# Hybrid attention and retention trunk: block corners, GpSimd pieces, adding transfers and the grouping of the FFN blocks

## The chip, the cores and the metric

The kernel runs on one core of a Trainium2 chip. The metric is device time in microseconds (us) of one execution. An execution of this program was also taken by the profiler, and its instructions, DMA packets and semaphores are what the views below are made from. TensorE (PE; its weight loads are PEld), VectorE (DVE), ScalarE (ACT), GpSimd (POOL) and SyncE (SP, which issues most DMA transfers) each work through a queue of their own in order.

## The reference

A decoder trunk of two layers on 512 tokens of width 1024, with 16 learned meta tokens in front (528 positions). All is float32.

```
h = concat(meta, x)                                        # (528, 1024)
for each of 2 layers:
    xn   = rmsnorm(h) ;  proj = xn @ w_in                  # 1024 x 3592
    fox  = 8 heads of 64: softmax(q k^T / 8 + c_t - c_s, causal) v,  c = cumsum(log sigmoid(gate))
    ret  = 4 heads of 128: rotary, sum over s<=t of gamma^(t-s) (q_t k_s) v_s, group norm, times silu(gate)
    h   += concat(fox, ret) @ w_out                        # 1024 x 1024
    hn   = rmsnorm(h)
    h   += (silu(hn @ w_gate) * (hn @ w_up)) @ w_down      # 1024 x 2816 x 1024
return rmsnorm(h) without the meta positions
```

In the second layer only the 512 real positions are needed behind the keys and values.

## The kernel before

**Layout and precision.** `h` lies transposed, eight tiles of 128 channels by 528 positions. Every float32 product is made as three products of a high and a low part (`hi*hi`, `hi*lo`, `lo*hi`): ScalarE rounds a tensor to its high part, and VectorE or GpSimd subtracts it from the original for the low part (`split`, line 126; `convert`, line 149, for the weights). TensorE's order is written out by hand as a list of steps (a plan), and the Tile framework orders the other engines' instructions in advance, by a model of their costs; each engine then runs its queue as it stands.

**Attention.** A dense step is one 128-channel piece of the contraction (`dense_steps`, line 180). While it runs, the next weight tile is converted in two halves of four pieces, at steps 1 and 4 (`ahead`). Where a job has `pool` set, GpSimd makes the low half of 128 x 512 elements in one instruction (line 177). The steps of the forgetting attention (`fox_steps`) and the retention (`ret_steps`) are merged between dense steps. A fox head takes its 512 real queries in blocks b = 0 to 3 of 128 (and the meta queries as b = -1 in layer 0). `scores` writes the probabilities of block b into the tile `p_tiles[b]`, with 16 + 128(b+1) keys and zeros behind them. `turn` (line 526) transposes them with TensorE in 128-key pieces 0 to b+1; the last piece holds 16 keys. Only the last 16 queries of the block can see those, so of this piece a corner of 16 x 16 is not zero. ScalarE and VectorE split the transposed pieces into `pth` and `ptl`, and `product` multiplies them by the values.

**FFN.** The 22 blocks of 128 FFN columns run in `ROUNDS`. The first `PLAIN` blocks of a layer are plain: gate and up product, each eight steps of full width. Every other block is a `Unit`: gate and up are made together by a scheme of seven instead of eight half-size products, on the two halves of the contraction (HB = 4 pieces each) and of the positions (w = 264 or 256). Its weights are four jobs: `make1` (the gate tile `a` itself), `make2` (S: the sum of the up tile's halves, and that minus a's first half), `make3` (a's first half minus b's) and `make4` (a's second half minus S). `load` fetches `a` and `b` by SP. The inputs' sums are made by `x_forms` (line 816), four times per layer, with tiles `S` of two buffers which `make2` uses too; their places among the plan's steps are fixed, before steps 12, 20, 28 and 36 of the FFN. `need` converts a job and up to two behind it. Converted weights lie in two rings of two buffers (`whi/wlo` and `fwhi/fwlo`), in turn. When a round is done, its down products are filled into the units of the next one, one pair of output pieces per unit: half of it in the middle, half after the unit's last product. The last round's down products stand alone; in the last layer they run in two column parts, and the closing norm is placed between their pieces (`after_a` to `after_7`).

The names the prediction uses: line 200 is the dense steps' matmul, 401 the transposes, 552 the attention's product with the values, 860 the units' matmul, 995 the down products', 177 the low halves, 849 the units' low parts, 894 and 895 the sums in `make2`, 901 the one in `make3`, 283 the end of a norm's Newton step, 1169 the closing norm's high part, 1091 its sums, 1095 its output products.

## Time and profile before

| | |
|---|---|
| three timed runs | 1282.78, 1283.13, 1283.19 us; median 1283.13 |
| profiled execution | span 1282.4 us; the median of the runs is 0.7 us above it |
| mean granted TensorE clock | 0.996 |
| busy: PE, DVE, ACT, POOL | 1265.5, 1013.6, 691.4, 177.3 us |
| HBM read / written | 116.91 MB / 2.13 MB |

A busy time is the union of an engine's instructions, so a matmul's modelled end that overlaps the next one counts once. The page and the other views name an instruction by its line, engine, operation and tiles (`out<-in`). "idle before" and "waited for" name what ended an engine's idle time.

### The profile page before, as it was taken

The page shows a single profiled execution, that of the slowest core. Times are in us where ns is not written, and L with a number is a line of the kernel's source. Part 1 is how long each engine was busy: PE and PEld are TensorE (multiplying, and loading weights), DVE is VectorE, ACT ScalarE, POOL GpSimd, SP SyncE. Part 2 cuts the span into 40 slices and gives each one's busy share as a digit, 9 for nine tenths or more (in the row PEclk, how much of TensorE's full clock was granted, in tenths as well). Part 3 has the DMA queues.
Part 4 walks back from the last instruction along what each step waited for, and adds up shares of the span by engine and source line. Part 5 has one row for each costly group of instructions (what it writes and reads, how often), then busy time and mean ns, then how long its engine had stood idle before and what let it go on. Part 6 is the DMA issues. An engine that isn't in the chain of part 4 may idle for free.

```text
span 1282.4 us, 23297 instructions
## 1 busy us (share of the span) xinstructions
PE 1265.5 (99%) x9335; PEld 1205.4 (94%) x9335; DVE 1013.6 (79%) x1828; ACT 691.4 (54%) x1246; POOL 177.3 (14%) x145
## 2 busy tenths in 40 slices
PE   9999999999999999999999999999999999999997
PEld 8899999999999999999999989999789999999996
DVE  7877856879988887887686878568899878888866
ACT  6666655676444444444455665457765444444444
POOL 1233333210000000000014334333000000000000
PEclk9999999999999999999999999999999999999998
DMA  6222222123333333332323122222223322332321
GB/s 231 76 67 84 75 84 84 60 68 121 109 98 99 99 99 99 100 99 83 99 76 117 59 99 84 75 92 67 99 78 129 106 99 99 99 100 99 105 77 66
DMA packets 45676, 120.54 MB, mean 94 GB/s; under 512 B 5360, under 2 KB 12272, under 8 KB 45568
## 3 DMA queue, kind: packets, MB, share of 16 engines
q1 hardware_dynamic: 45136, 118.77, 28.2%
q8 instruction: 73, 1.20, 0.4%
q14 instruction: 35, 0.29, 0.1%
q10 hardware_dynamic: 432, 0.29, 0.1%
HBM read 116.91 MB, written 2.13 MB: 93 GB/s over the span
## 4 chain that ended last, share of the span: by engine, by line
PE 88%; DVE 7%; ACT 3%; DMA 1%; issue 1%; DVEq 0%; ACTq 0%
PE psd L200 27%; PE psa L860 18%; PE psd L995 14%; PE psd L860 13%; PE psa L995 4%; PE psa L200 4%; PE psa L401 2%; PE psa L490 2%; PE psa L552 1%; PE psa L709 1%; PE psa L679 1%; DMA bc<-cdr 1%; ACT whi L176 0%; DVE qs L421 0%; DVE kl L435 0%
## 5 line engine op out<-in xcount | busy, mean ns | idle before, releaser
L177 POOL TENSOR_TENSOR wlo<-raw,whi 128x512 fp32r<-128x512 f32 x126 | 171.8, 1377 | 386.0 <-ACT whi L176 384.8
L200 PE MATMUL psd<-xh,whi 128*128 128x264 f32 (+1 forms) x792 | 196.6, 316 | 0.8 <-ACT whi L176 0.8
L200 PE MATMUL psd<-xh,wlo 128*128 128x264 f32 (+1 forms) x792 | 187.2, 304 | 0.0
L200 PE MATMUL psd<-xl,whi 128*128 128x264 f32 (+1 forms) x792 | 186.5, 303 | 0.4 <-DVE xl L303 0.4
L200 PEld LDWEIGHTS psd<-xh,whi 128*128 128x128 f32 x792 | 128.9, 190 | 5.6 <-ACT whi L176 1.5
L200 PEld LDWEIGHTS psd<-xh,wlo 128*128 128x128 f32 x792 | 127.5, 189 | 6.4 <-DVE wlo L177 0.4
L200 PEld LDWEIGHTS psd<-xl,whi 128*128 128x128 f32 x792 | 128.2, 190 | 4.7 <-DVE xl L303 0.8
L176 ACT CAST whi<-raw 128x512 fp32r<-128x512 f32 (+1 forms) x168 | 98.2, 614 | 38.2 <-PE psd L200 18.0
L848 ACT CAST whi<-raw 128x1024 fp32r<-128x1024 f32 (+2 forms) x62 | 54.9, 885 | 51.3 <-PE psd L860 40.0
L848 ACT CAST fwhi<-raw 128x1024 fp32r<-128x1024 f32 (+2 forms) x62 | 55.6, 897 | 47.5 <-PE psd L860 40.0
L849 DVE TENSOR_TENSOR wlo<-raw,whi 128x1024 fp32r<-128x1024 f32 (+2 forms) x62 | 62.9, 1014 | 11.3 <-ACT whi L848 10.9
L849 DVE TENSOR_TENSOR fwlo<-raw,fwhi 128x1024 fp32r<-128x1024 f32 (+2 forms) x62 | 64.0, 1032 | 9.0 <-ACT fwhi L848 8.7
L860 PE MATMUL psa<-th,whi 128*128 128x264 f32 (+1 forms) x232 | 65.5, 282 | 0.0
L860 PE MATMUL psa<-th,wlo 128*128 128x264 f32 (+1 forms) x232 | 65.4, 282 | 0.0
L860 PE MATMUL psa<-tl,whi 128*128 128x264 f32 (+1 forms) x232 | 65.3, 282 | 0.0
L510 ACT ACTIVATE pdNone<-pdNone,nmax 128x144 f32<-128x144 f32 (+1 forms) x64 | 36.9, 576 | 50.4 <-DVE nmax L497 33.6
L860 PE MATMUL psa<-th,fwhi 128*128 128x264 f32 (+1 forms) x224 | 63.4, 283 | 0.0
L860 PE MATMUL psa<-tl,fwhi 128*128 128x264 f32 (+1 forms) x224 | 63.3, 283 | 0.0
L860 PE MATMUL psa<-th,fwlo 128*128 128x264 f32 (+1 forms) x224 | 63.3, 282 | 0.0
L128 DVE TENSOR_TENSOR ptl<-psa,pth 128x512 fp32r<-128x512 f32 (+4 forms) x88 | 41.9, 490 | 26.9 <-ACT pth L127 26.9
L926 ACT COPY e<-psa 128x264 f32<-128x264 f32 (+1 forms) x114 | 42.8, 375 | 28.4 <-PE psa L860 24.1
L848 ACT CAST fwhi<-S 128x1024 fp32r<-128x1024 f32 x20 | 21.0, 1049 | 68.6 <-PE psa L860 66.5
(339 smaller groups left out, 4031.7 us busy)
## 6 DMA issues: line engine op xcount, KB each, us to landing
raw<-w_in SPq DMA_DIRECT2D x54, 512.0 KB, 3.5
raw<-w_gate SPq DMA_DIRECT2D x44, 512.0 KB, 3.9
fraw<-w_up SPq DMA_DIRECT2D x38, 512.0 KB, 3.5
raw<-w_down SPq DMA_DIRECT2D x64, 256.0 KB, 2.7
raw<-w_out SPq DMA_DIRECT2D x16, 512.0 KB, 3.5
raw<-w_down SPq DMA_DIRECT2D x32, 192.0 KB, 2.4
bc<-cdr SPq DMA_DIRECT2D x16, 264.0 KB, 3.2
raw<-w_up SPq DMA_DIRECT2D x6, 512.0 KB, 3.4
```

Of the source, the lines that this page charges most:

```text
L128: pin(nc.vector.tensor_sub(lo, src, hi.bitcast(F32)), pinned)
L176: pin(nc.scalar.copy(hi, job["raw"][:, c0:c1]), pinned)
L177: pin(sub(lo, job["raw"][:, c0:c1], hi.bitcast(F32)), pinned)
L200: nc.tensor.matmul(ps[1][b][:, 0:c1 - c0], w[:, wk, :], x[:, c0:c1], start=(k == 0 and i == 0), stop=(k == n - 1 and i == 2))
L401: nc.tensor.transpose(ps[:, 128 * j:128 * j + 128], src[:, o:o + 128], idt)
L490: nc.tensor.matmul(sc[0:nq, 0:c1 - c0], st["q"][s][:, q0:q0 + nq], kk[:, c0:c1], start=(i == 0), stop=(i == 1))
L510: nc.scalar.activation(pr, pr, AF.Exp, bias=nmax[0:nq], scale=-1.0, accum_out=rsum)
L848: nc.scalar.copy(hi, src)
L849: nc.vector.tensor_sub(lo, src, hi.bitcast(F32))
L860: nc.tensor.matmul(bank()[:, 0:b.shape[-1]], a[:, o + k, :], b, start=(fresh and k == 0 and i == 0), stop=(k == n - 1 and i == 2), skip_gr ...
L926: nc.scalar.copy(self.t["e"][:, i], self.t["x"][:, 0:w])
L995: nc.tensor.matmul(v[:, 0:c1 - c0], a[:, s * n + k, :], b[:, c0:c1], start=(k == 0 and i == 0), stop=(k == n - 1 and i == 2))
```

## The change

- **Rounds.** `PLAIN` 3 becomes 2, so block 2 of each layer is a unit. The first round has two blocks, the others four.
- **Corners.** The probabilities of the four blocks lie in one tile, shifted so that their ends stand in the same columns. `turn` transposes pieces 0 to b (piece 0 for the meta block). After block 3's exponentials VectorE transposes the four ends in one instruction of 32 x 32 blocks, and one split writes the four corners into the turned tiles. These two tiles stay for the whole attention part; the rest of the corner pieces is cleared once per layer, after the gates' and the first value's weights, which lie in the same space, are used.
- **GpSimd's pieces.** Low halves on GpSimd are made in four instructions of 128 columns.
- **Adding transfers.** A unit's `load` also fetches the up tile's second half into S, and two transfers issued by GpSimd add to what is loaded: a's first half to b's, and the up tile's first half to S. `make2` and `make3` lose one VectorE operation each. Signs are turned accordingly (S is negated while it is split, the second factor of the activation is negated, and `x_forms` uses a negated norm weight).
- The scratch for GpSimd-issued DMA descriptors is set to 4096 bytes.

```diff
-ROUNDS = ((0, 3), (3, 7), (7, 11), (11, 15), (15, 19), (19, 22))
-PLAIN = 3
+ROUNDS = ((0, 2), (2, 6), (6, 10), (10, 14), (14, 18), (18, 22))
+PLAIN = 2
+WP = 128 * NBLK + 32
 ...
-        for lst, n, cols, z0 in ((p_tiles, NBLK, None, None), (v_tiles, 2, TP, T)):
-            lst[:] = [phase["att"].tile([128, cols or 128 * (i + 2)], F32, name=f"pd{z0}_{i}") for i in range(n)]
-            for i, t in enumerate(lst):
-                z = META + 128 * (i + 1) if z0 is None else z0
-                zero(l, t[:, z:z + 128 - META])
+        probs = phase["att"].tile([128, NBLK, WP], F32, name="probs")
+        p_tiles[:] = [probs[:, b, 128 * (NBLK - 1 - b):WP] for b in range(NBLK)] + [probs]
+        zero(l, probs[:, :, WP - 32 + META:WP])
+        v_tiles[:] = [phase["att"].tile([128, TP], F32, name=f"vt{i}") for i in range(2)]
+        for t in v_tiles:
+            zero(l, t[:, T:TP])
+        turned[:] = [phase["att"].tile([128, 5, T], F32R, name=f"pt{i}") for i in range(2)]
 ...
+    def corners(i, rows):
+        c = T + 128
+        return turned[i].rearrange("p j t -> p (j t)")[0:rows, 5 * T - NBLK * c:5 * T].rearrange(
+            "p (b c) -> p b c", b=NBLK)[:, :, c - META:c]
+
+    def clear_corners(l):
+        for i in range(2):
+            zero(l, corners(i, 128).bitcast(F32))
 ...
-            pin(sub(lo, job["raw"][:, c0:c1], hi.bitcast(F32)), pinned)
+            step = 1 if job["pool"] else c1 - c0
+            for i in range(0, c1 - c0, step):
+                pin(sub(lo[:, i:i + step], job["raw"][:, c0 + i:c0 + i + step], hi[:, i:i + step].bitcast(F32)), pinned)
 ...
+            if b == NBLK - 1:
+                st["ct"] = tmp.tile([32, NBLK, 32], F32, name="ct", tag="ct")
+                nc.vector.transpose(st["ct"], p_tiles[NBLK][96:128, :, WP - 32:WP])
 ...
-            if b == blocks[0]:
-                st["pt"] = (at("pth", shape=(128, 5, T)), at("ptl", shape=(128, 5, T)))
-            pth, ptl = st["pt"]
+            pth, ptl = st["pt"] = turned
 ...
-            for j0, n, p3 in transpose_into(info[s, b], [128 * j for j in range(b + 2)]):
+            for j0, n, p3 in transpose_into(info[s, b], [128 * j for j in range(max(b + 1, 1))]):
                 split(pth[:, j0:j0 + n, q0:q0 + nq], ptl[:, j0:j0 + n, q0:q0 + nq], p3[:, :, 0:nq])
+            if b == NBLK - 1:
+                split(corners(0, 32), corners(1, 32), st["ct"][:, :, 32 - META:32])
 ...
-                nc.vector.scalar_tensor_tensor(s[:, 5], a[1], g1, s[:, 4], ALU.mult, ALU.subtract)
+                nc.vector.scalar_tensor_tensor(s[:, 5], a[1], neg[:, l * HB + k:l * HB + k + 1], s[:, 4], ALU.mult, ALU.add)
 ...
                         nc.sync.dma_start(self.t[n], src[l, self.f])
+                    s = self.t["s"] = fft("S", F32, (128, NK, 128), 2)
+                    nc.sync.dma_start(s[:, HB:NK], w_up[l, self.f][:, HB:NK])
+                    nc.gpsimd.dma_start(self.t["b"][:, 0:HB], w_gate[l, self.f][:, 0:HB], accum_op=ALU.add)
+                    nc.gpsimd.dma_start(s[:, HB:NK], w_up[l, self.f][:, 0:HB], accum_op=ALU.add)
 ...
             def make2(self, hi, lo):
-                a, b = self.t["a"], self.t["b"]
-                s = self.t["s"] = fft("S", F32, (128, NK, 128), 2)
-                nc.vector.tensor_add(s[:, HB:NK], b[:, 0:HB], b[:, HB:NK])
-                nc.vector.tensor_sub(s[:, 0:HB], s[:, HB:NK], a[:, 0:HB])
-                splits(hi, lo, s)
+                a, s = self.t["a"], self.t["s"]
+                nc.vector.tensor_add(s[:, 0:HB], s[:, HB:NK], a[:, 0:HB])
+                nc.scalar.activation(hi, s, AF.Copy, scale=-1.0)
+                nc.vector.scalar_tensor_tensor(lo, s, -1.0, hi.bitcast(F32), ALU.mult, ALU.subtract)
 ...
             def make3(self, hi, lo):
-                a, b = self.t["a"], self.t["b"]
-                nc.vector.tensor_sub(b[:, 0:HB], a[:, 0:HB], b[:, 0:HB])
-                splits(hi, lo, b)
+                splits(hi, lo, self.t["b"])
 ...
-                nc.vector.tensor_sub(a[:, HB:NK], a[:, HB:NK], s[:, 0:HB])
+                nc.vector.tensor_add(a[:, HB:NK], a[:, HB:NK], s[:, 0:HB])
 ...
-                nc.vector.scalar_tensor_tensor(u[:, c], sg[:, c], RSC, st["R"][:, c], ALU.mult, ALU.mult)
+                nc.vector.scalar_tensor_tensor(u[:, c], sg[:, c], -RSC, st["R"][:, c], ALU.mult, ALU.mult)
 ...
+    neg = const.tile([128, DEPTH * HB], F32, name="neg")
+    for i in range(DEPTH):
+        nc.vector.tensor_scalar_mul(neg[:, HB * i:HB * i + HB], vec[:, V_FFN + NK * i + HB:V_FFN + NK * i + NK], -1.0)
 ...
-        plan += v + [ropes]
+        plan += v + [lambda: clear_corners(l), ropes]
 ...
-    nc = bacc.Bacc("TRN2", target_bir_lowering=False, num_devices=1)
+    nc = bacc.Bacc("TRN2", target_bir_lowering=False, num_devices=1,
+                   dynamic_dma_scratch_size=4096)
```

More of the change, by code (lines that the diff above doesn't have):

```diff
@@ L64, in hybrid_kernel @@
     nc.vector.memset(onec, 1.0)
-    p_tiles, pm_tiles, v_tiles, end_tiles, low_keys = [], [], [], [], []
+    p_tiles, pm_tiles, v_tiles, end_tiles, low_keys, turned = [], [], [], [], [], []
     rot = {"pm": 0}
@@ L445, in own @@
         def own():
-            t = at("ptl", shape=(128, 2, NK, 128))
+            t = flat(1, 2 * NK * 128).rearrange("p (i k c) -> p i k c", i=2, k=NK)
             return t[:, 0], t[:, 1]
```

4 lines of the change are left out of this document (3 added, 1 removed).

## The prediction

> **What bounds the kernel now.** I read the page first, then the busy time in chosen stretches, then TensorE's waits, and last single stretches in order of time. The page:
>
> ```profile
> span 1282.4 us, 23297 instructions
> ...
> PE 1265.5 (99%) x9335; PEld 1205.4 (94%) x9335; DVE 1013.6 (79%) x1828; ACT 691.4 (54%) x1246; POOL 177.3 (14%) x145
> ```
>
> TensorE is busy for all but 17 us. The view by stretches gives, after each stretch's length, the busy us of PE, PEld, DVE, ACT and POOL: the start of layer 0's FFN, the middle of it, the middle of layer 1's, the start of layer 1's.
>
> ```profile
> 284.15:333.03 48.88, 48.88 (x405) 48.73 (x404) 48.77 (x83) 33.34 (x52) 0.00 (x0) 1.00 0.33 110
> 400.00:600.00 200.00, 200.00 (x1649) 200.00 (x1648) 161.01 (x236) 89.77 (x125) 0.00 (x0) 1.00 0.30 97
> 1000.00:1200.00 200.00, 200.00 (x1399) 186.74 (x1398) 164.31 (x236) 92.12 (x130) 0.00 (x0) 1.00 0.32 103
> 916.00:961.00 45.00, 44.63 (x203) 36.08 (x202) 44.41 (x74) 30.29 (x47) 0.00 (x0) 1.00 0.31 107
> ```
>
> In the middle of the FFN TensorE never idles and VectorE has a fifth of its time free. At the two FFN starts VectorE is full too (48.77 of 48.88, 44.41 of 45.00). So a matmul less is time won wherever VectorE keeps up, and the FFN starts are where it may not. Two of TensorE's few waits:
>
> ```profile
> PE psa L1119 <- ACT sqh L1169: 1.3, 1, 1.3
> PE psa L552 <- DVE ptl L128: 1.2, 1, 1.2
> ```
>
> **Part 1: matmuls removed.** A head now turns key pieces 0 to b of query block b, not 0 to b+1: four transposes less in each of 16 heads, 64 in all. TensorE in order of time:
>
> ```profile
> 888.92 0.71 PE L401 MATMUL psa<-idt,pdNone 128*128 128x128 f32 x5
> 889.38 0.48 PE L200 MATMUL psd<-xh,whi 128*128 128x512 f32 x1
> 889.70 0.39 PE L200 MATMUL psd<-xl,whi 128*128 128x512 f32 x1
> ```
>
> From the first transpose to the second matmul are 0.78 us, holding five transposes and one 512-column matmul. That matmul's pace is 16.59/72 = 0.23 us (next fence), so a transpose costs 0.55/5 = 0.11 us, and 64 of them 7.0 us.
>
> Plain blocks: f block 2 of each layer becomes a unit of seven products. Plain, it is 2 x 8 x 3 matmuls of full width (48, each counted as two halves in layer 0, so 96); a unit has 7 x 4 x 3 = 84 of half width. The chain of waits (start, us, what) gives the pace:
>
> ```profile
> 283.75 20.56 PE psd L200 x168
> ...
> 400.88 1.48 PE psd L860 x12
> ...
> 942.17 16.59 PE psd L200 x72
> ```
>
> ```profile
> 1050.42 1.42 PE psd L860 x12
> ```
>
> Layer 0: 20.56/168 = 0.122 us in plain blocks, 1.48/12 = 0.123 in units, so the 12 fewer save 1.5 us. Layer 1: 48 x 0.230 = 11.1 us against 84 x 1.42/12 = 9.9 us, 1.1 us saved. Together 2.6 us. The down products keep their count, since only the grouping of the 22 blocks changes. Removed in all: 9.6 us of TensorE.
>
> The corners' new work on VectorE (a 32-row transpose of 128 elements and a split of 64 per head) is costed at nothing: each head also drops 4 x 128 columns of splits, so the sum falls. Without that cover it would be some 0.4 us a head on an engine with a fifth of its time free. The clearing of the corners is two memsets of 64 elements a layer, behind the value product and under the next dense products.
>
> **Part 2: GpSimd in quarter pieces.** What a 512-column subtraction on GpSimd does to VectorE shows in one line of the code, whose 528- and 512-column instructions take (min/median/max ns):
>
> ```profile
> L283 DVE SCALAR_TENSOR_TENSOR r<-nwt,r x8: 671/692/1771, 93.2 to 905.0; 128x528 f32<-128x528 f32 x4, 128x512 f32<-128x512 f32 x4
> ```
>
> The longest, 1.1 us over the median, is the first, and in order of time it stands beside a GpSimd subtraction, which outlasts its own mean as well:
>
> ```profile
> 92.46 1.83 POOL L177 TENSOR_TENSOR wlo<-raw,whi 128x512 fp32r<-128x512 f32 x1 [3.41 <-ACT whi L176]
> 93.17 1.69 DVE L283 SCALAR_TENSOR_TENSOR r<-nwt,r 128x528 f32<-128x528 f32 x1
> ```
>
> GpSimd's own groups:
>
> ```profile
> L177 POOL TENSOR_TENSOR wlo<-raw,whi 128x512 fp32r<-128x512 f32 x126 | 171.8, 1377 | 386.0 <-ACT whi L176 384.8
> ...
> L99 POOL MEMSET pdNone<- 128x112 f32 x4 | 0.6, 185 | 0.0
> ```
>
> The Trainium skill, "SBUF — State Buffer", section "Who interferes with whom", says that a VectorE instruction with two SBUF inputs and a GpSimd instruction that reads SBUF exclude each other, and whichever starts first keeps the shared ports to its end. By this rule a blocked VectorE instruction would wait a quarter as long; the trace agrees: 1.69 us here against the median of 0.69.
>
> For the sum I take rows. A quarter piece costs between 1377/4 = 0.34 us (no cost of its own) and 0.53 us (with the 0.19 us of the shortest wide memset added), so four take 1.4 to 2.1 us in place of 1.4. GpSimd then works at most 126 x 0.74 = 93 us more, in attention alone, where it sits idle over half the time waiting for ScalarE's high halves. Its low halves are made a product ahead (steps 1 and 4 of 8), so up to 0.7 us later is covered; without that cover each of 126 would cost it. VectorE's blocked instructions get up to 0.8 us shorter. Only those on a chain gain: the wait of 1.2 us at line 552 above, and one or two like it. I take -1.5 us, between -4 (all of attention's short waits) and +2 (low halves late in a few places).
>
> **Part 3: the two adding transfers.** VectorE loses two 128x512 operations a unit, L894 and L901:
>
> ```profile
> L894 DVE TENSOR_TENSOR S<-fraw 128x512 f32<-128x512 f32 x38 | 26.3, 691 | 28.8 <-DMA fraw<-w_up 28.8
> ```
>
> That is 2 x 0.69 = 1.4 us a unit, off the path in the middle of the FFN (VectorE idles there) and so worth nothing by itself; it is worth its time at the FFN starts (part 4). The turned signs are the same operations with other operands. In exchange SP issues one load more a unit and GpSimd's queue two transfers, each behind a wait for the load it adds to. Behind them on GpSimd stands no computation until layer 1's zeroing and the last output product. The landings:
>
> ```profile
> fraw<-w_up SPq DMA_DIRECT2D x38, 512.0 KB, 3.5
> raw<-w_down SPq DMA_DIRECT2D x64, 256.0 KB, 2.7
> ...
> h<-x_t SPq DMA_DIRECT2D x8, 264.0 KB, 4.4
> ```
>
> No row shows an adding transfer. I bound one by 2.7 us (a plain one of its size) and 4.4 us (the slowest of about its size); I take 3.5, since it reads two operands. S is then ready after 2.7 + 3.5 = 6.2 us instead of 3.5 us. The splits that read S wait for a ring slot, not for it, so in the steady state I cost this at nothing. If that cover goes, VectorE stands still in its queue (rival B).
>
> **Part 4: the FFN starts, with a plain block less in front.** Layer 0 before, VectorE and TensorE in order of time:
>
> ```profile
> 324.34 1.25 DVE L128 TENSOR_TENSOR tl<-S,th 128x1056 fp32r<-128x1056 f32 x1
> ```
>
> ```profile
> 329.06 1.22 DVE L849 TENSOR_TENSOR fwlo<-S,fwhi 128x1024 fp32r<-128x1024 f32 x1
> ...
> 333.61 0.28 PE L860 MATMUL psa<-th,fwhi 128*128 128x264 f32 x1
> ```
>
> The first product on sums starts at 333.61; the last x form was split at 325.6, the weights' sums at 330.3. Without the block TensorE arrives 96 x 0.122 = 11.7 us earlier, at 321.9, and reads the last x form three chunks (9 matmuls, 1.1 us) later, at 323.0. Where the x forms stand among the steps is fixed (steps 12, 20, 28, 36), and the unit's head now begins at step 32, so its conversions come ahead of the last form. VectorE, full since 284, drops before that form the block's four 512-column halves and L894 (5 x 0.68 = 3.4 us) and takes on the head's split, L895 and the sums' split (1.22 + 0.68 + 1.22 = 3.1 us). The last form is then ready at about 325.3, 2.3 us late. The third form and the unit's S, now held from its load on, share two buffers, which leaves no slack. I take 2.5 us of stall, and the same in layer 1, whose start looks the same: +5 us. Bounds: 0 (VectorE's order shifts other work back) and 5 us each (the third split and the last plain block's three operations come first too).
>
> **Part 5: rounds.** Units with a fill of two down steps last 12 matmuls less than those with three, so 1.5 us less. VectorE's work in one of three (period, then busy us):
>
> ```profile
> 345.30:359.90 14.60, 12.39 (x20) 1.00 0.31 100
> ```
>
> Now 12.4 - 1.4 - 0.3 (a low half of 512 columns instead of 768) = 10.7 of 13.1 us: no fuller than before, so no cost. At the very end the last round has four steps instead of three, which gives ScalarE and VectorE a third more time per piece:
>
> ```profile
> 1268.34 1.38 POOL L1095 TENSOR_TENSOR th<-th,e 128x544 f32<-128x544 f32 x1 [359.93 <-DVE e L1115]
> ...
> 1268.72 1.26 DVE L1091 TENSOR_TENSOR S<-S,sq 128x240 f32<-128x240 f32 x1
> ...
> 1271.73 0.38 PE L1119 MATMUL psa<-sqh,ones 128*128 128x240 f32 x1 [1.27 <-ACT sqh L1169]
> ```
>
> The closing sums wait 1.27 us for the squares, because a sum that normally takes 0.4 sat behind GpSimd for 1.26. I take -1.5 us, between 0 and -2.1.
>
> **Sum.** -7.0 - 2.6 - 1.5 (attention) + 5 - 1.5 (end) = -7.6 us. The profiled span of 1282.4 becomes 1274.8; the runs' median lies 0.7 above the span, so **1275.5 us**. Its own range from the bounds is -15.7 to +2.4: 1267.4 to 1285.5.
>
> **Rivals.** A, *the starts are hidden*: VectorE's blocked time in attention and the 1.4 us a unit suffice. For it speaks that VectorE idles before 284; against it, that the h additions which open that stretch wait for TensorE. -7.0 - 2.6 - 2.1 - 3 = -14.7: 1268.4 us.
>
> B, *VectorE waits in its queue for the adding transfer*, slower: the order on VectorE is fixed in advance, and L894 today waits 28.8/38 = 0.76 us a unit for its load. With a second transfer of 2.7 to 4.4 us behind the first, that wait w becomes 1.5 us (planned as closely as the first) up to 5.2 (not planned for). Behind it stand the sums that empty PSUM. VectorE's slack is 2.4 us in the 8 units of two. One of four lasts (84 + 48) x 0.122 = 16.1 us, of which VectorE by the row 400 to 600 is busy 161/200, 13.0 us, now 11.6: slack 4.5 us, in 32 units. TensorE loses 8(w - 2.4) + 32(w - 4.5): the gain is gone from w = 3.4, and at 4.5 it is 17 us: 1292 us. "DMA: Bandwidth & Descriptors" of the Trainium skill (section "Anatomy of one DMA — SWDGE (gpsimd) path") fits such a transfer with 2.0 us plus its bytes at 436 GB/s, an estimate of 2.6 us for 256 KB, by which B would not come about; no run here shows one yet.
>
> C, *the starts eat it*: 5 us each, attention unchanged, 1 us at the end: -9.6 + 10 - 1 = -0.6: 1282.5 us, no change.
>
> **Chances.** Forecast 0.50, A 0.20, B 0.17, C 0.13. A measurement of this kernel tells 0.2% (2.6 us) from no change. Faster: 0.46 of the forecast, all of A, 0.04 of C: 0.70. Same: 0.12, the rest of both. Slower: B and a last 0.01: 0.18. The range 1267 to 1291 takes in the forecast's range, A, C and B up to w = 4.4.
>
> **What would show it.** Transposes 64 fewer and TensorE's busy time about 10 us less (part 1). VectorE's maximum at L283 below 1.2 us (part 2). No wait of VectorE on the sum of S over 2 us (part 3, against B). TensorE waiting 2 to 3 us for tl or a low half just after each FFN's plain blocks (part 4); none there means A, 5 us C. The closing sums not waiting for sqh (part 5). The forecast is wrong if TensorE idles in the middle of an FFN at all.

## The result and the profile after

The changed kernel takes **1301.3 us** (median of four runs, 1299.7 to 1304.2) against 1283.0 before: a ratio of 1.0142, 95% interval 1.0130 to 1.0155. It is 18 us slower. The prediction was 1275.5 us, 8 us faster, with a range up to 1291: both the number and the sign were wrong.

In the changed kernel the line numbers shift: 217 is the dense steps' matmul, 418 the transposes, 880 the units' matmul (and, through the same helper, that of the last down products of layer 1), 1016 the other down products', 142 and 143 the high and low part of a split, 841 to 845 an x form, 917 the unit's sum in S, 194 the low halves, 300 the end of the Newton step. Its page, head and busy times:

```profile
span 1299.3 us, 23968 instructions
...
PE 1265.1 (97%) x9319; PEld 1207.4 (93%) x9319; DVE 960.5 (74%) x1780; ACT 693.6 (53%) x1252; POOL 335.1 (26%) x602
```

VectorE has 53 us less to do, and TensorE 16 matmuls less, but TensorE now idles for 34 us where it idled for 17, and its busy time (1265.1 us) is that of before (1265.5): some of its matmuls take longer. Its longest waits (in all, times, longest):

```profile
PE psa L880 <- ACT th L142: 7.6, 2, 3.9
PE psa L880 <- ACT ah L142: 3.1, 1, 3.1
PE psd L1016 <- ACT ah L142: 2.1, 1, 2.1
PE psa L418 <- DVE vv L484: 1.8, 1, 1.8
PE psa L1261 <- DVE wide L61: 1.6, 1, 1.6
PE psa L880 <- DVE tl L143: 1.6, 2, 0.9
```

The first and the last row are the two FFN starts (the first unit waits for the fourth x form, th and tl), the second and third the ends of the two layers' FFNs (the last round's down products wait for the last unit's activations, ah). Before, no wait of these four stood in the profile. The stretches (length, busy us of PE, PEld, DVE, ACT, POOL, then granted clock, DMA share and GB/s) show what lies around them: the start of layer 0's FFN in three pieces, its middle, the ends of layer 0's and layer 1's, and the start of layer 1's.

```profile
316.00:320.00 4.00, 0.23 (x1) 0.19 (x1) 4.00 (x9) 1.80 (x3) 0.14 (x1) 1.00 0.42 131
320.00:325.00 5.00, 4.09 (x19) 3.94 (x19) 1.61 (x2) 1.57 (x3) 1.56 (x2) 0.52 0.91 222
325.00:330.00 5.00, 5.00 (x35) 5.00 (x35) 3.25 (x6) 0.75 (x2) 0.85 (x1) 0.80 0.90 197
```

```profile
400.00:600.00 200.00, 200.00 (x1645) 200.00 (x1645) 147.02 (x211) 89.91 (x125) 20.73 (x24) 1.00 0.54 145
```

```profile
625.00:640.00 15.00, 12.69 (x91) 12.27 (x90) 9.39 (x13) 7.46 (x10) 2.16 (x11) 0.89 0.36 107
1255.00:1268.00 13.00, 9.56 (x57) 8.58 (x56) 8.48 (x12) 6.42 (x8) 0.00 (x0) 0.91 0.09 33
950.00:965.00 15.00, 10.62 (x62) 9.96 (x62) 11.29 (x17) 7.58 (x12) 1.72 (x2) 0.78 0.51 136
```

Two things are to be seen. VectorE is busy for all of the 4 us in which TensorE stands (316 to 320). And the price does not end with the wait: behind it the granted clock is 0.52 and then 0.80 for ten microseconds, which costs, as an estimate from these rows, (1 - 0.52) x 5 + (1 - 0.80) x 5 = 3.4 us more. A stall of 3.9 + 0.9 us in layer 0 is thus some 8 us of time. The middle of layer 0's FFN is full, as before.

### The profile page after: what moved, and what is told of

It is laid out like the page before. It is cut to its first block, busy times and chain, and to the rows that moved or that the text cites. A ratio compares the mean times of both kernels' runs of the same rounds, so it can differ in the third digit from the quotient of the medians.

```text
span 1299.3 us, 23968 instructions
## 1 busy us (share of the span) xinstructions
PE 1265.1 (97%) x9319; PEld 1207.4 (93%) x9319; DVE 960.5 (74%) x1780; ACT 693.6 (53%) x1252; POOL 335.1 (26%) x602
## 4 chain that ended last, share of the span: by engine, by line
PE 84%; DVE 8%; DMA 3%; ACT 2%; issue 1%; DVEq 0%; ACTq 0%; SPq 0%; POOLq 0%
PE psd L217 25%; PE psa L880 18%; PE psd L1016 12%; PE psd L880 12%; PE psa L1016 4%; PE psa L217 4%; PE psa L418 2%; PE psa L572 2%; PE psa L507 1%; PE psa L729 1%; PE psa L699 1%; DMA S<-w_up 1%; DMA raw<-w_gate 1%; PE psa L379 1%; DMA bc<-cdr 1%
## 5 line engine op out<-in xcount | busy, mean ns | idle before, releaser
L194 POOL TENSOR_TENSOR wlo<-raw,whi 128x128 fp32r<-128x128 f32 x504 | 260.6, 552 | 294.8 <-ACT whi L191 294.7
L217 PE MATMUL psd<-xh,whi 128*128 128x264 f32 (+1 forms) x744 | 183.5, 315 | 0.1
L217 PE MATMUL psd<-xh,wlo 128*128 128x264 f32 (+1 forms) x744 | 174.0, 302 | 0.0
L908 POOL DMA_DIRECT2D S<-w_up x40 | 34.6, 864 | 301.8 <-DVE h L1023 219.8
L907 POOL DMA_DIRECT2D fraw<-w_gate x40 | 34.7, 868 | 257.0 <-DMA fraw<-w_up 162.3
L869 DVE TENSOR_TENSOR fwlo<-raw,fwhi 128x1024 fp32r<-128x1024 f32 (+1 forms) x64 | 65.4, 1021 | 39.2 <-ACT fwhi L868 39.2
L869 DVE TENSOR_TENSOR wlo<-raw,whi 128x1024 fp32r<-128x1024 f32 (+1 forms) x64 | 65.4, 1022 | 31.5 <-ACT whi L868 31.4
L868 ACT CAST fwhi<-raw 128x1024 fp32r<-128x1024 f32 (+1 forms) x64 | 56.9, 889 | 51.0 <-PE psd L880 43.2
L868 ACT CAST whi<-raw 128x1024 fp32r<-128x1024 f32 (+1 forms) x64 | 56.9, 889 | 43.5 <-PE psd L880 38.5
L527 ACT ACTIVATE probs<-probs,nmax 128x144 f32<-128x144 f32 (+1 forms) x64 | 36.9, 576 | 47.8 <-DVE nmax L514 35.0
```

Of the source, the lines that this page charges most:

```text
L194: pin(sub(lo[:, i:i + step], job["raw"][:, c0 + i:c0 + i + step], hi[:, i:i + step].bitcast(F32)), pinned)
L217: nc.tensor.matmul(ps[1][b][:, 0:c1 - c0], w[:, wk, :], x[:, c0:c1], start=(k == 0 and i == 0), stop=(k == n - 1 and i == 2))
L527: nc.scalar.activation(pr, pr, AF.Exp, bias=nmax[0:nq], scale=-1.0, accum_out=rsum)
L868: nc.scalar.copy(hi, src)
L869: nc.vector.tensor_sub(lo, src, hi.bitcast(F32))
L907: nc.gpsimd.dma_start(self.t["b"][:, 0:HB], w_gate[l, self.f][:, 0:HB], accum_op=ALU.add)
```

## The experiments

All times are medians, and each ratio is to the kernel before, run beside it on the same chip, with its 95% interval.

### Which part loses: the change taken apart

`old_rounds` puts rounds and plain blocks back:

```diff
-ROUNDS = ((0, 2), (2, 6), (6, 10), (10, 14), (14, 18), (18, 22))
-PLAIN = 2
+ROUNDS = ((0, 3), (3, 7), (7, 11), (11, 15), (15, 19), (19, 22))
+PLAIN = 3
```

> The changed kernel with the rounds and the three plain blocks of before put back, all else of the change kept. Theory: the loss sits wholly in the plain blocks and rounds. Without them the 64 transposes (-7.0 us) and the better attention (about -4.7 us by the two traces) remain: 1283 - 11.7 = 1271 us, and TensorE does not idle at the FFN starts or at the layer ends more than it did before. Rival 1, the adding transfers and GpSimd's 335 us (177 before) slow TensorE everywhere: 1283 - 9.6 + 26.5 less what little the rounds do, 1290 to 1300 us. Rival 2, my sum of before (-7.0 - 1.5): 1274.5 us.

1284.3 us, ratio 1.0008 (0.9999 to 1.0018). So the rounds cost 17 us, but my theory was wrong in the rest: 13 us of the expected gain are missing. VectorE's waits name the place:

```profile
DVE S L917 <- DMA S<-w_up: 15.9, 4, 5.0
```

In the changed kernel that row is 4.1, 4 times, 1.7 at most. `old_rounds_no_transfers` gives the two sums back to VectorE in `old_rounds`:

```diff
-                    s = self.t["s"] = fft("S", F32, (128, NK, 128), 2)
-                    nc.sync.dma_start(s[:, HB:NK], w_up[l, self.f][:, HB:NK])
-                    nc.gpsimd.dma_start(self.t["b"][:, 0:HB], w_gate[l, self.f][:, 0:HB], accum_op=ALU.add)
-                    nc.gpsimd.dma_start(s[:, HB:NK], w_up[l, self.f][:, 0:HB], accum_op=ALU.add)
...
+                s = self.t["s"] = fft("S", F32, (128, NK, 128), 2)
+                nc.vector.tensor_add(s[:, HB:NK], b[:, 0:HB], b[:, HB:NK])
...
+                nc.vector.tensor_add(b[:, 0:HB], a[:, 0:HB], b[:, 0:HB])
```

> The kernel old_rounds without the adding transfers: both weight sums are made by VectorE again, as before the change (two additions of 0.69 us a unit more, S taken only when they run). Theory: in old_rounds VectorE stood 15.9 us in front of the sum at L917 for the adding transfer of S, in 4 places of up to 5.0 us, all at the FFN starts, and TensorE lost 3.5 + 5.5 us behind it. Without the transfers those go, and the corners and pieces keep their gain: 1284.3 - 9 to -12 = 1272 to 1275 us. Rival: the loss is of GpSimd's pieces or of the corners, or VectorE's two more additions cost at the full starts what the transfers cost: 1281 to 1285 us.

1276.8 us, 0.9940 (0.9925 to 0.9955), a little above what I gave. `corners_alone` also takes GpSimd's pieces away (`step = c1 - c0`; the turned signs stay):

> The kernel before with the corners by VectorE alone (the signs of the sums, which cost nothing, stay turned): no adding transfers, GpSimd's low halves 512 columns wide, rounds and three plain blocks as before. Theory: 64 transposes of 0.11 us less, and VectorE's one corner transpose a step in their place: 1283 - 7 = 1276 us, and attention's further gain of about 5 us needs the 128-column pieces (then old_rounds_no_transfers is 3 to 5 us faster than this). Rival: the pieces do nothing and the further gain is the corners' (fewer splits for ScalarE and VectorE behind the transposes): 1271 to 1273 us, and the two kernels are equal.

1280.2 us, 0.9967 (0.9954 to 0.9980): 4 us above what I gave for the corners, but the pieces' part is as large as said. And `rounds_alone` is the kernel before with nothing but the new `ROUNDS` and `PLAIN = 2`:

> The kernel before with the new rounds and two plain blocks alone: no corners, no pieces, no adding transfers. By my recorded sum -2.6 + 5 - 1.5, 1284 us. By what the runs have shown since: VectorE is the fuller for its two additions a unit, TensorE arrives 11.7 us early and waits some 5 us in each start with a slowed clock behind it (8 us each), and the two layer ends lose 4.3 and 3.3 us for want of a leftover fill: 1283 - 2.6 + 16 + 7.6 = 1300 to 1306 us.

1306.8 us, 1.0182 (1.0166 to 1.0197), by the same waits as in the changed kernel: 7.1 us for th, 1.6 for tl, 3.1 and 2.1 for ah.

From the ratios, times 1283 us, the change adds up like this: corners -4.2, pieces -3.5, adding transfers +8.7, rounds and plain blocks +17.2; together +18.2. The intervals of `corners_alone` and `old_rounds_no_transfers` just touch, so how much of the first 7.7 us is the pieces' is known to some 2 us only. The shares also hold for this order of undoing alone: with the new rounds already in place the transfers cost only 2.7 us (`kept_fill` against `kept_fill_no_transfers` below, whose intervals touch), and `rounds_alone` loses 23 us where this sum has 17, probably because the stalls of both lie at the same FFN starts.

### Why the adding transfers lose

`old_rounds_s3` keeps them, but gives S a third buffer (in all three uses of the tag; the third, not shown, is in the closing norm):

```diff
-                s = fft("S", F32, (128, 6, w), 2)
+                s = fft("S", F32, (128, 6, w), 3)
-                    s = self.t["s"] = fft("S", F32, (128, NK, 128), 2)
+                    s = self.t["s"] = fft("S", F32, (128, NK, 128), 3)
```

> The kernel old_rounds with a third buffer for S, which the x forms and the units' sums share; all else, the adding transfers too, stays. Theory: the transfers are late at the starts only because the load into S must wait until an x form gives a buffer back (at 318.0 us the third form's low half ends, and S lands 5.2 us later); with a buffer more the load starts about one form earlier, and most of the 4.75, 4.28 and 4.97 us waits of VectorE go: 1284.3 - 6 to -10 = 1274 to 1278 us. Rival: the transfers are slow themselves (4.6 us median behind a load of 2.6 us, on a busier memory) or the queue they stand in is what is late: 1282 to 1285 us.

1276.0 us, 0.9936 (0.9921 to 0.9951): the theory held. In `old_rounds` VectorE, in order of time, at the start of layer 0's FFN:

```profile
316.72 1.26 DVE L143 TENSOR_TENSOR tl<-S,th 128x1056 fp32r<-128x1056 f32 x1
317.95 0.71 DVE L816 SCALAR_TENSOR_TENSOR sg<-psd,R 128x528 f32<-128x528 f32 x1
323.41 0.69 DVE L917 TENSOR_TENSOR S<-S,raw 128x512 f32<-128x512 f32 x1 [4.75 <-DMA S<-w_up]
```

The x form's split at 316.72 is the last reader of an S buffer, and only when it ends (317.98) can the next unit's load into S begin; load and adding transfer follow one another, VectorE stands in its queue for 4.75 us, and everything behind it with it. The median landings in the changed kernel:

```profile
S<-w_up SPq DMA_DIRECT2D x40, 256.0 KB, 2.6
S<-w_up POOLq DMA_DIRECT2D x40, 256.0 KB, 4.6
```

With the third buffer no wait on that transfer is left. But the time is then that of the kernel without the transfers: taking 1.4 us a unit from VectorE is worth nothing that can be measured. Nor is memory traffic the cause. The transfers read three pieces of 256 KB a unit more, 148.4 MB instead of 116.9 in the changed kernel, and the loads of 512 KB of `w_up` beside them land in 4.6 us instead of 3.5; `old_rounds_s3` keeps that traffic (146.8 MB, 4.8 us) and loses nothing by it.

### The layer ends

`kept_fill` is the changed kernel whose second unit of the last round takes no fill, so that one is left for the end:

```diff
-                if fills:
+                if fills and (f1, f) != (NF, f0 + 1):
```

> The changed kernel whose second unit of the last round in each layer takes no fill, so that its tail goes into the third unit and one fill of eight down steps is left over for the very end of the round, as before the change; counts of every operation stay. Theory: that leftover fill (48 half-width matmuls, some 5.8 us) is what used to cover the last unit's activation chain: the waits of 2.2 us in layer 0 and 3.3 us in layer 1 on the high half of the activations go, with the slowed matmuls behind them: 1301.3 - 6 to -10 = 1291 to 1295 us. Rival, a round of four is too much for ScalarE and VectorE whatever its order: the waits stay or move to the third unit's tail, 1299 to 1303 us.

1290.0 us, 1.0056 (1.0041 to 1.0070), 11 us less than the changed kernel, somewhat more than I gave. The waits for ah are gone, and the two stretches are full at full clock:

```profile
625.00:640.00 15.00, 15.00 (x126) 15.00 (x125) 11.54 (x17) 8.15 (x11) 0.00 (x0) 1.00 0.46 139
1255.00:1268.00 13.00, 13.00 (x108) 13.00 (x107) 8.04 (x18) 7.43 (x18) 0.00 (x0) 1.00 0.00 1
```

Most of the 11 us can be summed, as an estimate, from the changed kernel's rows: waits of 2.1 and 3.1 us for ah and 0.2 and 0.3 for its low half, and the slower clock, (1 - 0.89) x 15 + (1 - 0.91) x 13 = 2.8 us, together 8.5. The stretch behind the first end, 640 to 700 us, has a granted clock of 0.97, 1.8 us more; in `kept_fill` it is 1.00:

```profile
640.00:700.00 60.00, 57.49 (x416) 54.21 (x415) 38.39 (x75) 29.23 (x59) 18.89 (x37) 0.97 0.26 81
```

```profile
640.00:700.00 60.00, 58.15 (x433) 55.35 (x432) 40.43 (x84) 30.74 (x65) 21.21 (x41) 1.00 0.25 81
```

Before the change, three units met four fills, so behind the second half of the last unit's own fill a whole one (48 half-width matmuls in layer 0, 5.8 us) stood between that unit's tail and the first down product that reads its activations. Four units use up four fills, and only the half fill (24 matmuls, 2.9 us) is left to cover that chain. `plain2_old_rounds` takes the old `ROUNDS` with `PLAIN = 2`, which restores the leftover fill in another way:

> The changed kernel with two plain blocks but the rounds of before (block 2 is then a unit of the first round, and the last round again has three units for four fills). Theory: the FFN starts keep their stalls (7.9 us in layer 0, up to 11.6 us in layer 1), the two layer ends lose theirs (4.3 and 3.3 us, with the slower clock behind each): 1301.3 - 8 to -11 = 1290 to 1293 us, and no wait of TensorE on the low or high half of the activations above 1 us at the layer ends. Rival, the ends stall because a round of four is simply more for ScalarE and VectorE (not because no fill is left over): the same result here, told apart by the next kernel. Rival, the starts are all of it: 1300 us or more.

1296.5 us, 1.0098 (1.0082 to 1.0115). The ends are quiet here too (the closing sums wait 1.3 us, as before the change), but the starts are worse, 8.5 us for th and 2.6 for tl instead of 7.6 and 1.6, and waits of 3.7 us for ah and al come on top, which puts the time 3.5 us above what I gave. Why one unit more in the first round makes the wait for the fourth form longer was not followed up.

### The FFN starts: order, buffers or load

Three kernels try the order and the buffers. `forms_early` moves the x forms (`NK + 4 + 9 * i` becomes `NK + 4 + 5 * i`):

> The changed kernel with the four x forms put at steps 12, 17, 22 and 27 of the FFN instead of 12, 21, 30 and 39, so that all four come ahead of the first unit's load, which takes one of the two S buffers. Theory: in layer 0 the last form begins only when the third form's low half frees its S buffer, since the unit's S holds the other; with the forms ahead of the load the 5.2 us of TensorE's wait there and the 5.0 us in layer 1 go, mostly: 1301.3 - 8 to -14 = 1287 to 1293 us. Rival, VectorE is simply full there and a form put earlier pushes the plain blocks' own low halves back: TensorE waits as long, in the plain blocks instead of at the unit's middle, and the time stays at 1298 to 1304 us.

1301.6 us, 1.0145 (1.0130 to 1.0160): no gain, the time of the rival, though the wait isn't in the plain blocks, where the rival had it. It changed its name, not its size:

```profile
PE psa L880 <- ACT fwhi L918: 7.5, 2, 3.9
```

Now it is the unit's own sums that are late. `kept_fill_no_transfers` is `kept_fill` with the sums by VectorE:

> The kernel kept_fill (two plain blocks, rounds of 2 and 4, one fill kept for the end of the last round) without the adding transfers. Theory: S is then taken only when VectorE adds, not from the load on, so that the fourth x form finds a buffer; of kept_fill's stalls at the FFN starts (8.3 and 8.2 us) half or more goes, and what stays is VectorE's fullness: 1290 - 8 to -14 = 1276 to 1282 us. Rival 1, two plain blocks are too few cover whatever fills the buffers: 1286 to 1291 us. Rival 2, my recorded sum without any stall (rival A there): 1268 to 1272 us.

1289.1 us, 1.0035 (1.0023 to 1.0048); th 7.1 and tl 1.6 us, so rival 1. `kept_fill_s3` is `kept_fill` with the third S buffer:

> The kernel kept_fill (two plain blocks, rounds of 2 and 4, one fill kept for the end) with a third buffer for S, as in old_rounds_s3. Two causes of its stalls at the FFN starts stand against each other. Buffers: the fourth x form waits for the third's buffer; with one more the stalls (8.3 and 8.2 us with the slow clock behind them) go and the time is 1272 to 1277 us. VectorE full: it is busy without a gap from 310 to 320 us, while the first unit already needs the fourth form, so a buffer more changes the order of little: 1284 to 1290 us. After kept_fill_no_transfers I hold the second.

1297.4 us, 1.0108 (1.0093 to 1.0123): slower than `kept_fill`, which neither side expected. With a buffer free, the order planned for VectorE puts the unit's sum ahead of an x form's split, and the engine stands there:

```profile
305.28 0.69 DVE L917 TENSOR_TENSOR S<-S,raw 128x512 f32<-128x512 f32 x1 [3.84 <-DMA S<-w_up]
305.89 1.25 DVE L143 TENSOR_TENSOR tl<-S,th 128x1056 fp32r<-128x1056 f32 x1
```

The next two tried to take load from VectorE and give it to GpSimd. `kept_fill_s3_pool` and `old_rounds_s3_pool` let GpSimd make all low halves of the plain blocks:

```diff
-                    steps += dense_steps(w_gate[l, f], [(0, xs, NK, QC, g_done(f) if f else held.append)], banks=f == 1)
-                    steps += dense_steps(w_up[l, f], [(0, xs, NK, QC, u_done(f))])
+                    steps += dense_steps(w_gate[l, f], [(0, xs, NK, QC, g_done(f) if f else held.append)], True, banks=f == 1)
+                    steps += dense_steps(w_up[l, f], [(0, xs, NK, QC, u_done(f))], True)
```

> The kernel kept_fill_s3 whose plain blocks' low halves are made by GpSimd (idle there) in its 128-column pieces, instead of by VectorE: some 8 low halves of 0.61 to 0.68 us a layer, about 5 us, leave VectorE ahead of the fourth x form. Theory (VectorE full): TensorE's wait for th and tl falls by about that, from 5.2 us to under 1 us, and with it the slowed clock: 12 to 16 us faster than kept_fill_s3, 1270 to 1276 us. Rival (the order of the forms or their buffers decides, not VectorE's load): no change from kept_fill_s3 by more than 3 us. Rival 2: GpSimd's pieces are too slow for the plain blocks (a half-block of 4 pieces at 0.55 us, 2.2 us, against 24 half-width matmuls, 2.9 us) and TensorE waits for them instead.

> The kernel old_rounds_s3 with the plain blocks' low halves by GpSimd as well. There TensorE does not wait at the FFN starts, so by the theory VectorE's relief buys nothing: within 2 us of old_rounds_s3, 1274 to 1278 us. If GpSimd's pieces are too slow for a plain block, or reading SBUF from both engines slows VectorE, it is slower: 1279 us or more. Against kept_fill_s3_pool it tells what the second unit-made block is worth when nothing stalls (2.6 us by my recorded sum).

1299.7 us, 1.0129 (1.0114 to 1.0144), and 1303.2 us, 1.0156 (1.0139 to 1.0173): the second is 27 us slower than `old_rounds_s3`. In the first, the groups of GpSimd between 295 and 330 us (count, busy us, mean ns):

```profile
L194 POOL TENSOR_TENSOR wlo<-raw,whi 128x128 fp32r<-128x128 f32 x18 | 14.0, 1027 | 0.0
```

A piece takes 1.03 us there, 0.46 at the median of the whole run. Four of them are 4.1 us, more than the 2.9 us in which TensorE uses them up; and VectorE's split of an x form rises from 1.25 to 1.50 us beside them. VectorE's wait for S is longer as well (16.5 us in 3 places, 8.8 us in 2 in `kept_fill_s3`). So these two runs have several causes in them and decide nothing on load; `half_pool_no_transfers` is cleaner, without transfers and with the second halves (columns 512 to 1023) alone on GpSimd:

> The kernel kept_fill_no_transfers whose plain blocks' second low halves (columns 512 to 1023 of each weight) are made by GpSimd in 128-column pieces, with the first halves left to VectorE: about 4 x 0.61 = 2.4 us a layer leave VectorE, and GpSimd has two halves' time (5.8 us of TensorE) for each. By the load theory the wait for th and tl falls by 2.4 us a layer plus the slowed clock it brings: 1289 - 5 to -10 = 1279 to 1284 us. If GpSimd's pieces slow VectorE by as much as they relieve it (with all halves on GpSimd, VectorE's split of an x form rose from 1.25 to 1.50 us), 1287 to 1292 us.

1288.4 us, 1.0035 (1.0021 to 1.0049): equal to `kept_fill_no_transfers`. The waits for th are 9.5 us, longer. The planned order put a sum of the unit (916) ahead of the second plain block, and the fourth form's split stayed where it was (321.32 against 321.44 us).

`light_forms` takes the stall away. It leaves VectorE's four additions out of every x form of `kept_fill_no_transfers`:

```diff
-                nc.vector.tensor_sub(s[:, 2], s[:, 1], s[:, 0])
-                for i in range(2):
-                    nc.vector.scalar_tensor_tensor(s[:, 3 + i], b[1], g1, s[:, 1 + i], ALU.mult, ALU.subtract)
-                nc.vector.scalar_tensor_tensor(s[:, 5], a[1], neg[:, l * HB + k:l * HB + k + 1], s[:, 4], ALU.mult, ALU.add)
                 th, tl = (t[:, k % 2] for t in st["t"][k // 2])
-                split(th, tl, s[:, 2:6])
+                src = s[:, 0:2].unsqueeze(1).broadcast_to([128, 2, 2, w])
+                th, tl = (t.rearrange("p (i j) c -> p i j c", i=2) for t in (th, tl))
+                split(th, tl, src)
```

> The kernel kept_fill_no_transfers with VectorE's sums left out of the x forms: each form's halves are split from the two scaled blocks themselves, so that 1.8 us of VectorE's four additions a form, 7.2 us a layer, are not computed (the output is then not the reference's); ScalarE's scaling, both splits, their sizes and all matmuls stay. Load theory: the fourth form is ready up to 7 us earlier, the wait for th and tl (5.3 us in layer 0, some 6 us in layer 1) goes, and with it the slowed clock: 1289 - 14 to -17 = 1272 to 1275 us. Order theory: the fourth form still stands behind the unit's sums and the second plain block's work in VectorE's queue, TensorE still waits over 3 us there: 1283 to 1289 us.

1269.6 us, 0.9901 (0.9884 to 0.9917): 17 us less by the ratios, the most that the load theory gave. Layer 0's start, in `kept_fill_no_transfers` and then here:

```profile
310.00:320.00 10.00, 6.72 (x52) 6.10 (x50) 10.00 (x16) 4.99 (x8) 0.00 (x0) 1.00 0.05 16
320.00:330.00 10.00, 7.83 (x40) 7.54 (x41) 7.25 (x12) 3.40 (x5) 0.00 (x0) 0.66 0.35 117
```

```profile
310.00:320.00 10.00, 10.00 (x85) 10.00 (x84) 9.66 (x16) 5.14 (x8) 0.00 (x0) 1.00 0.38 120
320.00:330.00 10.00, 10.00 (x84) 10.00 (x84) 10.00 (x17) 4.51 (x7) 0.00 (x0) 1.00 0.19 47
```

Shapes, the number of buffers, the forms' places in TensorE's plan and the matmuls are the same; the additions left out are 7.2 us of VectorE's work a layer, and no wait of TensorE is left there. So the forms' work on VectorE makes the stall. But the run changes more than the load. The third form's split, the fourth form's scaling and first addition, and its split in `kept_fill_no_transfers`, then the third and fourth splits in `light_forms`:

```profile
311.43 1.25 DVE L143 TENSOR_TENSOR tl<-S,th 128x1056 fp32r<-128x1056 f32 x1
312.72 0.74 ACT L841 ACTIVATE S<-h,vec 128x528 f32<-128x528 f32 x1 [1.59 <-DVE tl L143]
317.96 0.42 DVE L842 TENSOR_TENSOR S<-S 128x264 f32<-128x264 f32 x1
321.44 1.25 DVE L143 TENSOR_TENSOR tl<-S,th 128x1056 fp32r<-128x1056 f32 x1
```

```profile
299.49 1.26 DVE L143 TENSOR_TENSOR tl<-S,th 128x1056 fp32r<-128x1056 f32 x1 [0.15 <-ACT th L142]
308.18 1.25 DVE L143 TENSOR_TENSOR tl<-S,th 128x1056 fp32r<-128x1056 f32 x1
```

The fourth split comes 13 us earlier, more than the 7.2 us left out: the planned order moved the forms ahead of other work, and VectorE, still nearly full (9.66 of 10 us, then 10.00), does that work later. In `kept_fill_no_transfers` the scaling waited 1.59 us until the third split gave a buffer of S back, and VectorE then came to the form only 4.5 us after the scaling's end. Load, order and buffers are thus not separated; two plain blocks without transfers and with a third S buffer were not run. How a kernel that computes everything could take the stall away was not found: which of GpSimd's slowness and the planned order spoils each attempt is only argued from single rows.

### A version that beats both

The two `last_four` kernels take what gained: three plain blocks, corners, pieces, a last round of four with a fill kept (as in `kept_fill`).

```diff
+ROUNDS = ((0, 3), (3, 6), (6, 10), (10, 14), (14, 18), (18, 22))
+PLAIN = 3
```

> The kernel old_rounds_s3 with rounds of 3, 3, 4, 4, 4 and 4, three plain blocks as before, and the second unit of the last round without a fill, so that a fill is left for its end. Part 5 of the prediction gave a last round of four 1.5 us (0 to 2.1). In old_rounds_s3 TensorE loses 3.1 us after 1250 us, in kept_fill, which has this end, 1.2: I expect 1.5 to 2 us less, 1276.0 - 1.5 to -2 = 1274 to 1274.5 us. If ScalarE and VectorE do not fill the last round's gaps with the time, 1276 us again; if a round of three units with four fills, one round earlier, loses what the end gains, 1276 to 1278 us.

> The kernel last_four_s3 without the adding transfers and with two buffers for S (old_rounds_no_transfers with that other order of rounds). If the adding transfers are worth nothing once they are not late (old_rounds_s3 0.9936 and old_rounds_no_transfers 0.9940 of the time before), it takes the same as last_four_s3 within 1 us, 1274 to 1275.5 us. If their 1.4 us of VectorE a unit count at the new end, it is 1 to 2 us slower than last_four_s3.

1275.3 us, 0.9941 (0.9926 to 0.9956), and **1274.0 us, 0.9929 (0.9915 to 0.9944)**: 9 us faster than before, 27 than the changed kernel. Neither differs from `old_rounds_no_transfers` (0.9940) or `old_rounds_s3` by more than the intervals, so the gain of the new end isn't shown in the time. The trace has it: in both, TensorE no longer waits after 1240 us at all, where it waited 1.3 us before. And without the transfers it is no slower than with them.

## Why the prediction was wrong

**Part 1, transposes: right on TensorE, too much in time.** The transposes of a head's key pieces fell from 224 to 160, and in `corners_alone` TensorE's busy time from 1265.5 to

```profile
PE 1258.2 (99%) x9271; PEld 1197.6 (94%) x9271; DVE 1016.4 (80%) x1845; ACT 687.5 (54%) x1246; POOL 177.3 (14%) x144
```

-7.3 us where I had -7.0. The kernel's time fell by 4.2 us (2.6 to 5.9): part came back as waits, above all in the first head, where the values' product waited 1.8 us for a split of the transposed pieces instead of 1.2. "Costed at nothing" for the corners was nearly right on VectorE's sum (1016 against 1014 us, where I had said that it falls) and wrong in that one place. In the changed kernel itself TensorE's busy time fell by 0.4 us and not by 10, because the matmuls behind the stalls are slower. The 2.6 us for block 2 as a unit could not be measured by themselves, since no complete kernel runs it without a stall; `light_forms`, which does, took 1269.6 us. That this is near rival A's 1268.4 is luck, since it also leaves out work.

**Part 2, pieces: right in direction, undersized.** -3.5 us where I had -1.5. Line 300 (283 before), whose longest was 1771 ns:

```profile
L300 DVE SCALAR_TENSOR_TENSOR r<-nwt,r x8: 673/700/853, 88.5 to 908.0; 128x528 f32<-128x528 f32 x4, 128x512 f32<-128x512 f32 x4
```

Below 1.2 us, as said. A piece took 0.55 us on average (0.46 at the median), just above the bounds of 0.34 to 0.53. The low halves of the keys show that nothing was saved, only cut up (before; then the changed kernel):

```profile
L435 DVE TENSOR_TENSOR kl<-tq,kh x16: 669/705/1692, 35.7 to 832.3; 64x528 fp32r<-64x528 f32 x16
```

```profile
L452 DVE TENSOR_TENSOR kl<-tq,kh x16: 671/872/973, 33.9 to 836.8; 64x528 fp32r<-64x528 f32 x16
```

The median rises, the longest falls from 1.69 to 0.97 us, and the sum stays (13.5 and 13.7 us). That no single instruction of a chain is late by a microsecond any more is the likely gain; it is argued from these rows, not shown.

**Part 3, adding transfers: right for the middle, wrong for the starts.** In the steady state they cost nothing, as costed, and in the changed kernel VectorE's waits on the sum of S stayed under 2 us (1.7 at most), as said. But I also held that VectorE's relief "is worth its time at the FFN starts". There they cost 8.7 us with three plain blocks (`old_rounds` against `old_rounds_no_transfers`), and 2.7 us with two (`kept_fill` against `kept_fill_no_transfers`, whose intervals touch). The failed step is the claim that the splits "wait for a ring slot, not for it": at the starts the load waits for an S buffer, and VectorE for the load. The transfer itself was undersized too, 4.6 us where I took 3.5 and bounded it by 4.4. The Trainium skill's "DMA: Bandwidth & Descriptors" (section "Anatomy of one DMA — SWDGE (gpsimd) path") gave an estimate of 2.6 us for it, which the trace does not bear out for a transfer that adds. Rival B had the mechanism, VectorE waiting in its queue for the transfer, but placed it in the middle of the FFN, where it did not come about.

**Part 4, FFN starts: the place and the wait were right, the size was not.** This is the step that failed most: the term of +5 us, 2.5 us a layer and at most 5. The waits alone were 4.8 us in layer 0 and 4.4 in layer 1, still inside the bound, though longer than the 2.5 I took. VectorE in the changed kernel, in order of time:

```profile
316.35 0.43 DVE L842 TENSOR_TENSOR S<-S 128x264 f32<-128x264 f32 x1
316.69 0.89 DVE L844 SCALAR_TENSOR_TENSOR S<-h,vec,S 128x264 f32<-128x264 f32 x2
317.50 0.71 DVE L143 TENSOR_TENSOR al<-tq,ah 128x528 fp32r<-128x528 f32 x1
318.12 0.49 DVE L845 SCALAR_TENSOR_TENSOR S<-h,neg,S 128x264 f32<-128x264 f32 x1
318.52 0.69 DVE L869 TENSOR_TENSOR fwlo<-raw,fwhi 128x512 fp32r<-128x512 f32 x1
319.12 0.69 DVE L928 TENSOR_TENSOR raw<-raw,S 128x512 f32<-128x512 f32 x1
319.75 1.26 DVE L143 TENSOR_TENSOR tl<-S,th 128x1056 fp32r<-128x1056 f32 x1
```

Three operations of the plain block and the unit (al at 143, 869 and 928, 2.1 us) stand inside the fourth form, which my 2.5 us had counted as one stretch. The larger miss is that a wait was priced as its own length: with the clock behind it, it is some 8 us in layer 0. In layer 1 the clock of 0.78 over 15 us adds 3.3 us to the waits of 4.4, and a wait of 1.5 us on sg, at 974 us, follows. The two starts thus cost some 17 us, an estimate from these rows, where the sum had 5; taking the forms' additions away gave as much (17 us, `light_forms`). I had named the two S buffers as the thing without slack. In the changed kernel and in `kept_fill_no_transfers` the fourth form's scaling did wait for one, 0.34 and 1.59 us, but most of the delay behind it is VectorE's queue; more on the buffers is not shown.

**Part 5, rounds: one half right, the other missing.** Units of two steps cost nothing that a run shows, as said, and the closing sums no longer wait for sqh (-1.5 in the sum). Not seen at all was that a fill of the last round had stood behind its last unit and covered its activations. "Only the grouping of the 22 blocks changes" was nearly true of the counts (layer 1's last round, cut into two column parts, has one block more and so 24 more and narrower matmuls: 9295 in `last_four_no_transfers`, 9271 in `old_rounds_no_transfers`), but not of the cover. In place of -1.5 us the ends cost 11.

"The forecast is wrong if TensorE idles in the middle of an FFN at all" came about only just. Layer 0's middle is full; in layer 1's TensorE waits 1.1 us, once, for h (line 1016, at 1026 us):

```profile
1000.00:1200.00 200.00, 198.88 (x1395) 185.73 (x1394) 148.96 (x211) 92.35 (x131) 22.47 (x26) 1.00 0.58 156
```

The 18 us were not lost there.

## What to carry to other kernels

Price a stall of TensorE of two microseconds or more at its length plus the slow matmuls behind it, at layer 0's FFN start here 1.7 times its length (8.2 us for 4.8). When a loop is regrouped, list not only how many steps there are but which of them stands between the last producer and its first reader; a count that stays can hide a cover that goes. And a transfer that takes work off an engine also takes a buffer for its whole flight: ask who held that buffer before.

## What the runs showed of the hardware

In the changed kernel the four waits of 2 to 4 us were each followed by a lower granted clock or slower matmuls. Behind the wait of 2.1 us at the end of layer 0 the down products ran at half pace for some 3 us (TensorE in order of time, two matmuls a row; start to start a pair takes 0.24 us before):

```profile
631.31 0.40 PE L1016 MATMUL psd<-ah,wlo 128*128 128x264 f32 x2
633.79 0.51 PE L1016 MATMUL psd<-ah,whi 128*128 128x264 f32 x2 [2.08 <-ACT ah L142]
634.53 0.81 PE L1016 MATMUL psd<-al,whi 128*128 128x264 f32 x2 [0.23 <-DVE al L143]
635.14 0.64 PE L1016 MATMUL psd<-ah,wlo 128*128 128x264 f32 x2
635.58 0.64 PE L1016 MATMUL psd<-ah,whi 128*128 128x264 f32 x2
636.02 0.64 PE L1016 MATMUL psd<-al,whi 128*128 128x264 f32 x2
```

A pair then takes 0.44 us. The Trainium skill's "TensorE: Matmul & The Clock Gate" (section "What's actually happening") gives half clock after an idle window of about 3.4 us; the slower pace (0.44 us against 0.24) agrees, but here a wait of 2.1 us was enough.

GpSimd and VectorE slow each other, and GpSimd the more: in `kept_fill_s3_pool` a 128-column piece, 0.46 us at the median, took 1.03 us on average between 295 and 330 us, where VectorE was busy for 27 of the 35 us, and VectorE's split of an x form took up to 1.50 us instead of 1.25. The Trainium skill's "SBUF — State Buffer" (section "Who interferes with whom") names the port that the two share; that both slow down agrees with it. In these runs, work moved from VectorE to an idle GpSimd did not relieve VectorE: its busy time was 959.3 us in `kept_fill_s3` and 961.1 in `kept_fill_s3_pool` with 16 instructions fewer, 951.2 and 954.2 in `old_rounds_s3` and `old_rounds_s3_pool` with 24 fewer, 1007.1 and 1006.9 in `kept_fill_no_transfers` and `half_pool_no_transfers` with 8 fewer.
